# A rotation's 64 powers from two 8-entry tables instead of five doublings, in a hybrid S5, attention and mLSTM trunk

## Chip, cores and metric

The kernel runs on one core of a Trainium2 chip. The metric is the device time of one execution in microseconds (us): the median of three runs before the change is 1186.29 us, with runs from 1185.99 to 1187.22 us.

## The reference, cut to what matters

Two residual layers on a sequence of 512 positions and 1024 channels, all in float32. Layer 0 mixes with an S5 state-space head group and a dilated attention side by side, layer 1 with an mLSTM; a squared-ReLU MLP follows each. What the change touches is the S5 recurrence:

```python
lam_bar = jnp.exp(lam * dt)                       # 32 groups x 64 complex states
b_bar = ((lam_bar - 1.0) / lam)[..., None] * lax.complex(b_re, b_im)
bu = jnp.einsum('bsgc,gpc->bsgp', u32.astype(jnp.complex64), b_bar)
_, states = lax.associative_scan(s5_combine, (a_el, bu), axis=1)   # x[t] = lam_bar*x[t-1] + bu[t]
y = jnp.einsum('bsgp,gcp->bsgc', states, c).real + d * u32
```

The kernel cuts the 512 positions into 64 blocks of 8. Within a block everything is small matrices; between blocks the state is multiplied by lam_bar to the 8th power. That complex factor is split into its size (mag8) and its angle. The angle is taken out by a rotation with the powers 0 to 63 of the unit number cos + i sin of 8 angles, so that a real scan (size only) runs along the 64 blocks, and then put back. The change is about how these 64 powers are made.

## The kernel before

**Layout.** Activations lie as 8 tiles of 128 channels by 512 positions. Every projection weight block (a "unit", 128 x 1024 floats) is loaded by SP's queue and split in two parts whose sum is the weight: ScalarE copies the high part (`wh`, the line of copy_act, L120), VectorE subtracts to get the low part (`wl`, L96). TensorE multiplies three combinations (24 matmuls of 512 columns for a unit). There are two slots for `wh` and two for `wl` in layer 0, so a unit's copy can start when the unit that held its slot has been multiplied.

**Order of the work.** `EVEN_SEQ` is the hand-written order of layer 0's steps; a planner then reorders instructions by readiness, with the program's order as priority, and fixes each engine's queue. Each engine runs its queue strictly in that order. The start of the sequence is

```python
"u0 C0 a0 K0 E0 b0 u1 n0 T0 a2 C1 u2 E1 v0 v1 K1 C2 u3 E2 v2 B0 B1 v3 O0 ..."
```

The steps u, a, b, v are projections and take the weight units in this order: u0, a0, b0, u1, a2, u2, v0, v1, u3, v2, v3. The v steps share four PSUM accumulators, from v0 to the end of v3, and these four are all there are of that kind; u3, which comes before v2 in the order, needs one of them, so TensorE runs u3 after v3, and u3's split weight keeps its slot until then.

**S5.** The 32 groups are worked in four rounds Q of 8 groups: C (the powers for the input matrix), K (the same for the output, `CG`), T (matrices from them), E (the rotation), B (rotate, scan, rotate back), O (output). `s5_params` (called in the middle of the loading loop, before the sixth of the 8 `prep` calls) makes what all rounds share: `lrr`, `lsr`, `mag8`, the start values `e1`, and, with 25 small instructions on GpSimd (POOL), five repeated squarings of the unit number, `pr` and `pis`. After them POOL makes the tables `la` and `lb` for K.

`s5_rot` (step E) runs once for each round. It fills power 0, copies power 1, and then doubles the list five times: each doubling is two products and a sum on VectorE, followed (for the first four) by two ScalarE copies that swap the halves of the partitions, because real parts lie in partitions 0 to 63 and imaginary parts in 64 to 127 of `A`, and the other way round in `S`. The last step is four ScalarE copies of 64 x 512 from `A` into the tile `E`. `A` and `S` are the tiles x6 and x7, shared by all rounds.

Of the kernel before, what the change touches and what calls it, by code (L numbers as in the profile page):

```python
# [12 lines left out]
AF = mybir.ActivationFunctionType  # L13
ALU = mybir.AluOpType
AX = mybir.AxisListType

P = 128
# [44 lines left out]
class Trunk:  # L62
# [425 lines left out]
    def s5_params(self, pool):  # L488
        G = 32
        u = lambda name, shape=(P, G): self.t(pool, shape, "s5_" + name)  # L490
        lp = Slab([self.tmp("rA", bufs=1), self.tmp("rB", bufs=1), self.tmp("qs", bufs=1)])
        prm = self.prm
        are, aim, ldt = prm[:, 0], prm[:, 1], prm[:, 2]
        w = lambda name, shape=(P, G): lp.get(shape)
        dt = w("dt")
        self.exp_acc(lp, dt, ldt)
        z = w("z", (P, 2, G))
        th = w("th", (P, 2, G))
        self.mul(z[:, 0], are, dt)
        self.ts(z[:, 1], z[:, 0], 8.0, ALU.mult)  # L500
        self.mul(th[:, 0], aim, dt)
        self.ts(th[:, 1], th[:, 0], 8.0, ALU.mult)
        mag = w("mag", (P, 2, G))
        self.exp_acc(lp, mag, z)
        sn = w("sn", (P, 2, G))
        cs = w("cs", (P, 2, G))
        self.sincos(lp, sn, cs, th)
        lre = self.tmp("qv", bufs=1)[:, 0:9 * G].rearrange("p (i g) -> p i g", g=G)
        lim = self.tmp("sf")[:, 0:9 * G].rearrange("p (i g) -> p i g", g=G)
        lrr = u("lrr", (P, 8, G))  # L510
        lsr = u("lsr", (P, 8, G))
        self.nc.vector.memset(lre[:, 0], 1.0)
        self.nc.vector.memset(lim[:, 0], 0.0)
        self.mul(lre[:, 1], mag[:, 0], cs[:, 0])
        self.mul(lim[:, 1], mag[:, 0], sn[:, 0])
        for n in (1, 2, 4):
            mk = lp.mark()
            t1 = lp.get((P, n, G))
            t2 = lp.get((P, n, G))
            sr = lre[:, 1:1 + n]  # L520
            si = lim[:, 1:1 + n]
            br = lre[:, n:n + 1].to_broadcast([P, n, G])
            bi = lim[:, n:n + 1].to_broadcast([P, n, G])
            self.mul(t1, sr, br)
            self.mul(t2, si, bi)
            self.sub(lre[:, n + 1:2 * n + 1], t1, t2)
            self.mul(t1, sr, bi)
            self.mul(t2, si, br)
            self.add(lim[:, n + 1:2 * n + 1], t1, t2)
            lp.reset(mk)  # L530
        for j in range(8):
            self.copy_act(lrr[:, j], lre[:, 7 - j])
            self.act(lsr[:, j], lim[:, 7 - j], AF.Copy, scale=self.sgn)
        mag8 = u("mag8")
        self.copy_act(mag8, mag[:, 1])
        e1 = u("e1", (P, 2, G))
        self.copy_act(e1[0:64, 0], cs[0:64, 1])
        self.copy_act(e1[64:128, 0], sn[64:128, 1])
        self.copy_act(e1[0:64, 1], sn[0:64, 1])
        self.copy_act(e1[64:128, 1], cs[64:128, 1])  # L540
        pr = u("pr", (P, 5, G))
        pis = u("pis", (P, 5, G))
        gt = lambda o, x, y, op: self.nc.gpsimd.tensor_tensor(out=o, in0=x, in1=y, op=op)  # L543
        mk = lp.mark()
        t1 = lp.get((P, G))
        t2 = lp.get((P, G))
        for m in range(5):
            cr = cs[:, 1] if m == 0 else pr[:, m - 1]
            ci = sn[:, 1] if m == 0 else pis[:, m - 1]
            gt(t1, cr, cr, ALU.mult)  # L550
            gt(t2, ci, ci, ALU.mult)
            gt(pr[:, m], t1, t2, ALU.subtract)
            gt(t1, cr, ci, ALU.mult)
            gt(pis[:, m], t1, t1, ALU.add)
        lp.reset(mk)
        self.ts(pis, pis, self.sgn, ALU.mult)
        lm = w("lm")
        nr = w("nr")
        ni = w("ni")
        den = w("den")  # L560
        kre = w("kre")
        kim = w("kim")
        t1 = w("kt1")
        self.ts(lm, lre[:, 1], 1.0, ALU.subtract)
        gt(nr, lm, are, ALU.mult)
        gt(t1, lim[:, 1], aim, ALU.mult)
        gt(nr, nr, t1, ALU.add)
        gt(ni, lim[:, 1], are, ALU.mult)
        gt(t1, lm, aim, ALU.mult)
        gt(ni, ni, t1, ALU.subtract)  # L570
        gt(den, are, are, ALU.mult)
        gt(t1, aim, aim, ALU.mult)
        gt(den, den, t1, ALU.add)
        self.nc.vector.reciprocal(out=den, in_=den)
        gt(kre, nr, den, ALU.mult)
        gt(kim, ni, den, ALU.mult)
        krs, kis, kr, kn = w("krs"), w("kis"), w("kr"), w("kn")
        self.ts(krs, kre, self.sgn, ALU.mult, -1.0, ALU.mult)
        self.ts(kis, kim, self.sgn, ALU.mult, -1.0, ALU.mult)
        self.ts(kn, kim, -1.0, ALU.mult)  # L580
        la, lb = u("la", (P, 9, G)), u("lb", (P, 9, G))
        bk = lambda k: k.unsqueeze(1).to_broadcast([P, 9, G])
        t9 = lp.get((P, 9, G))
        gt(la, lre, bk(krs), ALU.mult)
        gt(t9, lim, bk(kis), ALU.mult)
        gt(la, la, t9, ALU.subtract)
        gt(lb, lre, bk(kn), ALU.mult)
        gt(t9, lim, bk(kre), ALU.mult)
        gt(lb, lb, t9, ALU.subtract)
        self.lrr, self.lsr = lrr, lsr  # L590
        self.mag8, self.e1, self.pr, self.pis = mag8, e1, pr, pis
        self.la, self.lb = la, lb

    def ypair(self, k):
# [2 lines left out]
    def xt(self, k):  # L597
        return self.t(self.cp, (P, T), f"x{k}", F32, 1)

    def s5_rot(self, pool, Q):  # L600
        nc = self.nc
        gs = slice(8 * Q, 8 * Q + 8)
        v3 = lambda t: t.rearrange("p (g k) -> p g k", k=64)
        A, S = v3(self.xt(6)), v3(self.xt(7))
        nc.vector.memset(A[0:64, :, 0:1], 1.0)
        nc.vector.memset(A[64:128, :, 0:1], 0.0)
        nc.vector.memset(S[0:64, :, 0:1], 0.0)
        nc.vector.memset(S[64:128, :, 0:1], 1.0)
        self.copy_act(A[:, :, 1], self.e1[:, 0, gs])
        self.copy_act(S[:, :, 1], self.e1[:, 1, gs])  # L610
        for m in range(1, 6):
            n = 1 << m
            b = lambda x: x[:, m - 1, gs].unsqueeze(2).to_broadcast([P, 8, n])
            w = self.t(pool, (P, 8, n), "w0")
            self.mul(A[:, :, n:2 * n], A[:, :, 0:n], b(self.pr))
            self.mul(w, S[:, :, 0:n], b(self.pis))
            self.add(A[:, :, n:2 * n], A[:, :, n:2 * n], w)
            if m < 5:
                self.copy_act(S[0:64, :, n:2 * n], A[64:128, :, n:2 * n])
                self.copy_act(S[64:128, :, n:2 * n], A[0:64, :, n:2 * n])  # L620
        E = self.t(pool, (P, 2, 8, 64), "E", bufs=2)
        self.copy_act(E[0:64, 0], A[0:64])
        self.copy_act(E[64:128, 0], A[0:64])
        self.act(E[0:64, 1], A[64:128], AF.Copy, scale=-1.0)
        self.copy_act(E[64:128, 1], A[64:128])
        self.s5e[Q] = E
# [772 lines left out]
```

## Time and profile before

| what | value |
|---|---|
| median of 3 runs | 1186.29 us |
| time of the profiled execution | 1185.93 us |
| its span | 1184.1 us |
| TensorE matmul busy | 1161.5 us (98%) |
| VectorE busy | 813.4 us (69%) |
| ScalarE busy | 643.1 us (54%) |
| GpSimd busy | 64.1 us (5%) |
| mean granted TensorE clock | 0.995 |

All times in the rows are microseconds from the span's start. In the rows PE is TensorE, DVE is VectorE, ACT is ScalarE, POOL is GpSimd. "acc<-wh,hg" reads: written tile acc, read tiles wh and hg. Layer 0's mixer ends near 220 us; the rest of the span holds the MLPs and the mLSTM layer, and the change does not touch them. The stage that matters lies between 38 and 140 us.

### The profile page before, as it was taken

To read this page: it belongs to the slowest core of one execution; us is meant where nothing else is said; L and a number is where in the kernel's file an instruction comes from. 1 tells how busy PE (TensorE), PEld (TensorE's weight loads), DVE (VectorE), ACT (ScalarE), POOL (GpSimd) and SP (SyncE) were. 2 spreads that over 40 slices of the span, in tenths; PEclk is the share of its full clock that TensorE was granted. 3 is DMA by queue.
4 is the path that set the end of the run, shared out by engine and by line. 5 is a ranking of instruction groups with operands and counts; after the bars stand their busy time and mean duration, and the time that the engine had idled before them with its cause. 6 is when DMAs were issued, how large, how long until landed. Compare 5 with 4: busy or idle time off the path is not lost.

```text
span 1184.1 us, 15701 instructions
## 1 busy us (share of the span) xinstructions
PE 1161.5 (98%) x5540; PEld 956.2 (81%) x5540; DVE 813.4 (69%) x1466; ACT 643.1 (54%) x1162; POOL 64.1 (5%) x121
## 2 busy tenths in 40 slices
PE   6989999999999999999999999999999999999998
PEld 5868776788888888888888888887888888888887
DVE  8799864666457447779858975865664574477796
ACT  5467777444434446666656645544444444456664
POOL 0522220000000000000100000000000000000000
PEclk9989999999999999999999999999999999999999
DMA  6434531359999335565624333222599994346654
GB/s 236 125 95 122 143 79 58 121 202 370 351 345 357 122 120 160 194 195 172 188 90 153 107 108 107 81 89 72 182 353 367 345 350 144 111 157 195 208 185 158
DMA packets 73869, 216.56 MB, mean 183 GB/s; under 512 B 16888, under 2 KB 17992, under 8 KB 73792
## 3 DMA queue, kind: packets, MB, share of 16 engines
q1 hardware_dynamic: 72576, 214.27, 53.7%
q0 software_dynamic: 1216, 1.31, 0.5%
q8 instruction: 43, 0.70, 0.2%
q14 instruction: 34, 0.28, 0.1%
HBM read 175.14 MB, written 38.31 MB: 180 GB/s over the span
## 4 chain that ended last, share of the span: by engine, by line
PE 92%; DVE 3%; ACT 1%; POOL 1%; issue 1%; DMA 1%; SPq 0%; DVEq 0%; ACTq 0%
PE acc L123 79%; PE psa L123 8%; PE psb L123 3%; DVE wl L96 1%; PE psb L898 1%; POOL rA L543 1%; PE psb L281 1%; ACT wh L120 0%; ACT hg L117 0%; DVE hg L108 0%; DMA hg<-in_amask 0%; DMA wr<-in_w_l 0%; DVE x L108 0%; PE psb L1207 0%; DVE x L96 0%
## 5 line engine op out<-in xcount | busy, mean ns | idle before, releaser
L123 PE MATMUL acc<-hg,wh 128*128 128x512 f32 x1600 | 500.7, 393 | 8.8 <-ACT hg L117 7.2
L120 ACT ACTIVATE wh<-wr 128x1024 fp32r<-128x1024 f32 x243 | 257.2, 1060 | 398.1 <-PE acc L123 321.3
L96 DVE TENSOR_TENSOR wl<-wr,wh 128x1024 fp32r<-128x1024 f32 x243 | 297.3, 1224 | 221.5 <-ACT wh L120 211.4
L123 PEld LDWEIGHTS acc<-hg,wh 128*128 128x128 f32 x1600 | 298.7, 188 | 70.1 <-ACT hg L117 7.2
L123 PE MATMUL acc<-hg,wl 128*128 128x512 f32 x800 | 313.6, 392 | 0.6 <-DVE wl L96 0.6
L123 PE MATMUL acc<-wh,sp 128*128 128x512 f32 x768 | 223.0, 389 | 0.0
L123 PEld LDWEIGHTS acc<-hg,wl 128*128 128x128 f32 x800 | 150.7, 188 | 31.9 <-DVE wl L96 1.1
L123 PEld LDWEIGHTS acc<-wh,sp 128*128 128x128 f32 x768 | 144.2, 188 | 30.0
L123 PE MATMUL acc<-wl,sp 128*128 128x512 f32 x384 | 135.9, 390 | 0.8 <-DVE wl L96 0.8
L120 ACT ACTIVATE sp<-s 128x256 fp32r<-128x256 f32 x224 | 89.8, 409 | 6.8 <-PE acc L123 5.7
L96 DVE TENSOR_TENSOR tq<-tq,tq 128x1024 f32<-128x1024 f32 x64 | 78.2, 1222 | 21.0 <-DMA tq<-in_w2s 20.0
L96 DVE TENSOR_TENSOR sp<-s,sp 128x256 fp32r<-128x256 f32 x224 | 86.8, 417 | 1.4 <-ACT sp L120 1.4
L123 PEld LDWEIGHTS acc<-wl,sp 128*128 128x128 f32 x384 | 71.9, 188 | 16.6 <-DVE wl L96 1.6
L123 PE MATMUL acc<-wh,hg 128*128 128x512 f32 x192 | 63.0, 402 | 5.4 <-ACT wh L120 5.4
L123 PEld LDWEIGHTS acc<-wh,hg 128*128 128x128 f32 x192 | 36.6, 193 | 13.2 <-ACT wh L120 5.8
L123 PE MATMUL psa<-wh,sp 128*128 128x512 f32 x128 | 42.0, 389 | 0.0
L117 ACT ACTIVATE rr<-acc 128x512 f32<-128x512 f32 x72 | 41.6, 578 | 0.0
L117 ACT ACTIVATE s<-rr 128x512 f32<-128x512 f32 x64 | 40.4, 631 | 1.0
L123 PE MATMUL acc<-wl,hg 128*128 128x512 f32 x96 | 38.5, 401 | 0.3 <-DVE wl L96 0.3
L108 DVE SCALAR_TENSOR_TENSOR sf<-zb,cvw,sf 128x512 f32<-128x512 f32 x48 | 35.3, 747 | 2.3 <-ACT sf L117 1.8
L96 DVE TENSOR_TENSOR x<-x,acc 128x512 f32<-128x512 f32 x16 | 10.8, 686 | 29.3 <-PE acc L123 29.2
L123 PE MATMUL acc<-y,wh 128*128 128x512 f32 x96 | 30.0, 394 | 0.0
(324 smaller groups left out, 1327.7 us busy)
## 6 DMA issues: line engine op xcount, KB each, us to landing
wr<-in_w_l SPq DMA_DIRECT2D x67, 512.0 KB, 3.5
wr<-in_w SPq DMA_DIRECT2D x64, 512.0 KB, 5.2
tq<-in_w2s SPq DMA_DIRECT2D x64, 512.0 KB, 6.3
T<-tq SPq DMA_DIRECT2D x64, 512.0 KB, 4.8
wr<-T SPq DMA_DIRECT2D x64, 512.0 KB, 3.3
wr<-in_w2s SPq DMA_DIRECT2D x48, 512.0 KB, 4.0
x<-in_xT SPq DMA_DIRECT2D x16, 256.0 KB, 4.1
na<-scr SPq DMA_DIRECT2D x8, 256.0 KB, 3.7
```

What stands on the lines that cost most here:

```text
L96: return self.nc.vector.tensor_tensor(out=o, in0=x, in1=y, op=op)
L108: return self.nc.vector.scalar_tensor_tensor(out=o, in0=x, scalar=s, in1=y, op0=op0, op1=op1)
L117: return self.nc.scalar.activation(o, x, f, bias=bias, scale=scale, **kw)
L120: return self.nc.scalar.activation(o, x, AF.Copy)
L123: return self.nc.tensor.matmul(o, l, r, start=start, stop=stop)
L281: self.nc.tensor.transpose(p[:, k * P:(k + 1) * P], self.x[4 * n + k][:, t * P:(t + 1) * P], self.ident)
L543: gt = lambda o, x, y, op: self.nc.gpsimd.tensor_tensor(out=o, in0=x, in1=y, op=op)
L898: self.nc.tensor.transpose(t[:, k * P:(k + 1) * P], p[:, k * P:(k + 1) * P], self.ident)
```

## The change

The start values `e1` and the doublings in `s5_rot` go. `s5_params` keeps the five squarings on POOL (now called `sqr` and `sqi`, in temporary space) and calls the new `s5_tabs`, which makes, once for all 32 groups, a table of the powers 0 to 7 (`C8`, `S8`) and a table of the powers 0, 8, ..., 56 (`T1`, `T2`), each by two doublings with half swaps. Each round then forms its 64 powers as two products of 512 elements, one with each pair of tables, and their sum. Scratch is in the tiles x0 and x1.

```diff
-        e1 = u("e1", (P, 2, G))
-        self.copy_act(e1[0:64, 0], cs[0:64, 1])
         ...
-        self.ts(pis, pis, self.sgn, ALU.mult)
+        self.s5_tabs(pool, cs, sn, sqr, sqi)
+    def s5_tabs(self, pool, cs, sn, sqr, sqi):
+        self.ts(sqi, sqi, self.sgn, ALU.mult)
+        ...
+        for k, A, S, c, s in ((0, A8, S8, cs[:, 1], sn[:, 1]), (1, self.T1, S64, sqr[:, 2], sqi[:, 2])):
+            nc.vector.memset(A[up, :, 0:1], 1.0)
+            nc.vector.memset(A[dn, :, 0:1], 0.0)
+            nc.vector.memset(S[up, :, 0:1], 0.0)
+            nc.vector.memset(S[dn, :, 0:1], 1.0)
+            sc = lambda h: 1.0 if k == 0 else self.sgn[h]
+            self.copy_act(A[up, :, 1], c[up])
+            self.act(A[dn, :, 1], s[dn], AF.Copy, scale=sc(dn))
+            self.act(S[up, :, 1], s[up], AF.Copy, scale=sc(up))
+            self.copy_act(S[dn, :, 1], c[dn])
+            for m in (1, 2):
+                n = 1 << m
+                i = m - 1 + 3 * k
+                b = lambda x: x[:, i].unsqueeze(2).to_broadcast([P, G, n])
+                self.mul(A[:, :, n:2 * n], A[:, :, 0:n], b(sqr))
+                self.mul(tm[:, :, 0:n], S[:, :, 0:n], b(sqi))
+                self.add(A[:, :, n:2 * n], A[:, :, n:2 * n], tm[:, :, 0:n])
+                self.copy_act(S[up, :, n:2 * n], A[dn, :, n:2 * n])
+                self.copy_act(S[dn, :, n:2 * n], A[up, :, n:2 * n])
+        self.copy_act(self.C8[up], A8[up])
+        ...
+        self.act(self.T2, S64, AF.Copy, scale=self.sgn)
     def s5_rot(self, pool, Q):
-        for m in range(1, 6):
-            n = 1 << m
-            b = lambda x: x[:, m - 1, gs].unsqueeze(2).to_broadcast([P, 8, n])
-            w = self.t(pool, (P, 8, n), "w0")
-            self.mul(A[:, :, n:2 * n], A[:, :, 0:n], b(self.pr))
-            self.mul(w, S[:, :, 0:n], b(self.pis))
-            self.add(A[:, :, n:2 * n], A[:, :, n:2 * n], w)
-            if m < 5:
-                self.copy_act(S[0:64, :, n:2 * n], A[64:128, :, n:2 * n])
-                self.copy_act(S[64:128, :, n:2 * n], A[0:64, :, n:2 * n])
+        A, W = self.xt(6), self.xt(7)
+        ta = lambda t: t[:, gs].unsqueeze(3).to_broadcast([P, 8, 8, 8])
+        tb = lambda t: t[:, gs].unsqueeze(2).to_broadcast([P, 8, 8, 8])
+        self.mul(v4(A), ta(self.T1), tb(self.C8))
+        self.mul(v4(W), ta(self.T2), tb(self.S8))
+        self.add(A, A, W)
```

## Rows read from the trace of the kernel before

**Rows 1.** The page's first part: busy time, share of span, instructions.
```profile
PE 1161.5 (98%) x5540; PEld 956.2 (81%) x5540; DVE 813.4 (69%) x1466; ACT 643.1 (54%) x1162; POOL 64.1 (5%) x121
```

**Rows 2.** TensorE's waits, 0 to 212 us: total, times, longest.
```profile
PE acc L123 <- ACT wh L120: 5.4, 1, 5.4
```

**Rows 3.** Chain of waits in order of time: start us, us, what.
```profile
38.15 0.43 POOL rA L543 x2
...
91.81 5.48 PE acc L123 x24
...
134.26 3.82 DMA hg<-in_amask
```

**Rows 4.** Busy by stretch: length, PE, PEld, DVE, ACT, POOL, PEclk, DMA, GB/s.
```profile
60.00:70.00 10.00, 4.34 (x10) 2.86 (x10) 9.84 (x28) 5.19 (x12) 3.08 (x2) 0.68 0.27 77
70.00:100.00 30.00, 30.00 (x196) 25.57 (x195) 28.52 (x71) 22.35 (x46) 6.46 (x12) 0.99 0.40 120
100.00:134.00 34.00, 34.00 (x207) 30.01 (x207) 33.57 (x72) 23.70 (x43) 5.57 (x6) 1.00 0.49 138
```

**Rows 5.** TensorE timeline: start us, us, instruction, count, [idle before <-releaser].
```profile
59.79 0.39 PE L123 MATMUL acc<-wh,hg 128*128 128x512 f32 x1
65.57 2.07 PE L123 MATMUL acc<-wh,hg 128*128 128x512 f32 x4 [5.39 <-ACT wh L120]
67.91 0.79 PE L123 MATMUL acc<-wl,hg 128*128 128x512 f32 x1 [0.27 <-DVE wl L96]
...
73.48 0.39 PE L123 MATMUL acc<-wh,hg 128*128 128x512 f32 x1
...
75.31 1.04 PE L649 MATMUL psb<-cst,Z 128*128 128x128 f32 x8
```

**Rows 6.** ScalarE timeline, 53 to 66 us.
```profile
53.51 0.47 ACT L120 ACTIVATE x<-x 64x32 f32<-64x32 f32 x2 [1.59 <-DVE x L96]
55.99 0.52 ACT L120 ACTIVATE x<-x 64x64 f32<-64x64 f32 x2 [2.01 <-DVE x L96]
57.84 0.63 ACT L120 ACTIVATE x<-x 64x128 f32<-64x128 f32 x2 [1.32 <-DVE x L96]
...
59.07 1.04 ACT L120 ACTIVATE wh<-wr 128x1024 fp32r<-128x1024 f32 x1
61.27 1.27 ACT L120 ACTIVATE E<-x 64x512 f32<-64x512 f32 x2 [1.16 <-DVE x L96]
...
64.47 1.04 ACT L120 ACTIVATE wh<-wr 128x1024 fp32r<-128x1024 f32 x1
```

**Rows 7.** GpSimd timeline, 53 to 64 us.
```profile
53.46 0.82 POOL L543 TENSOR_TENSOR s_la<-qv,rB 128x288 f32<-128x288 f32 x1
...
59.08 3.16 POOL L800 TENSOR_TENSOR qky<-qkv,pwh 128x16 f32<-128x16 f32 x1 [1.43 <-DVE qkv L108]
62.22 0.86 POOL L543 TENSOR_TENSOR s_lb<-s_lb,rB 128x288 f32<-128x288 f32 x1
```

**Rows 8.** VectorE timeline, 48 to 73 us.
```profile
48.51 0.30 DVE L112 TENSOR_SCALAR s_pis<-s_pis,cst 128x160 f32<-128x160 f32 x1 [0.81 <-POOL s_pis L543]
...
55.99 0.80 DVE L96 TENSOR_TENSOR x<-x,s_pr 128x128 f32<-128x128 f32 x1
...
60.82 0.41 DVE L96 TENSOR_TENSOR x<-x,w 128x256 f32<-128x256 f32 x1
...
65.35 0.17 DVE L96 TENSOR_TENSOR x<-x,s_pr 128x16 f32<-128x16 f32 x1
...
68.94 0.22 DVE L96 TENSOR_TENSOR x<-x,s_pr 128x64 f32<-128x64 f32 x1
...
69.21 0.68 DVE L96 TENSOR_TENSOR w<-bin,s_lsr 128x512 f32<-128x512 f32 x1
...
70.55 0.28 DVE L96 TENSOR_TENSOR x<-x,s_pr 128x128 f32<-128x128 f32 x1
...
71.62 0.55 DVE L96 TENSOR_TENSOR Z<-Z,w 128x384 f32<-128x384 f32 x1
72.09 0.41 DVE L96 TENSOR_TENSOR x<-x,s_pr 128x256 f32<-128x256 f32 x1
```

More of the change, by code (lines that the diff above doesn't have):

```diff
@@ L535, in s5_params @@
         self.copy_act(mag8, mag[:, 1])
-        e1 = u("e1", (P, 2, G))
-        self.copy_act(e1[0:64, 0], cs[0:64, 1])
[L538 to L542, printed above, removed]
         gt = lambda o, x, y, op: self.nc.gpsimd.tensor_tensor(out=o, in0=x, in1=y, op=op)
+        sqr, sqi = w("sqr", (P, 5, G)), w("sqi", (P, 5, G))
         mk = lp.mark()
@@ L547, in s5_params @@
         for m in range(5):
-            cr = cs[:, 1] if m == 0 else pr[:, m - 1]
-            ci = sn[:, 1] if m == 0 else pis[:, m - 1]
+            cr = cs[:, 1] if m == 0 else sqr[:, m - 1]
+            ci = sn[:, 1] if m == 0 else sqi[:, m - 1]
             gt(t1, cr, cr, ALU.mult)
             gt(t2, ci, ci, ALU.mult)
-            gt(pr[:, m], t1, t2, ALU.subtract)
+            gt(sqr[:, m], t1, t2, ALU.subtract)
             gt(t1, cr, ci, ALU.mult)
-            gt(pis[:, m], t1, t1, ALU.add)
+            gt(sqi[:, m], t1, t1, ALU.add)
         lp.reset(mk)
-        self.ts(pis, pis, self.sgn, ALU.mult)
+        self.s5_tabs(pool, cs, sn, sqr, sqi)
         lm = w("lm")
@@ L590, in s5_params @@
         self.lrr, self.lsr = lrr, lsr
-        self.mag8, self.e1, self.pr, self.pis = mag8, e1, pr, pis
+        self.mag8 = mag8
         self.la, self.lb = la, lb
@@ L598, in xt @@
         return self.t(self.cp, (P, T), f"x{k}", F32, 1)
+    def s5_tabs(self, pool, cs, sn, sqr, sqi):
+        nc, G = self.nc, 32
+        tab = lambda name: self.t(pool, (P, G, 8), "s5_" + name)
+        self.C8, self.S8, self.T1, self.T2 = [tab(n) for n in ("c8", "s8", "t1", "t2")]
+        up, dn = slice(0, 64), slice(64, 128)
+        self.ts(sqi, sqi, self.sgn, ALU.mult)
+        w3 = self.xt(0).rearrange("p (n g e) -> p n g e", n=2, e=8)
+        A8, S8 = w3[:, 0], w3[:, 1]
+        w3 = self.xt(1).rearrange("p (n g e) -> p n g e", n=2, e=8)
+        S64, tm = w3[:, 0], w3[:, 1]
+        for k, A, S, c, s in ((0, A8, S8, cs[:, 1], sn[:, 1]), (1, self.T1, S64, sqr[:, 2], sqi[:, 2])):
[18 more added lines that the diff above has]
+        self.copy_act(self.C8[up], A8[up])
+        self.copy_act(self.C8[dn], S8[dn])
+        self.copy_act(self.S8[up], S8[up])
+        self.copy_act(self.S8[dn], A8[dn])
+        self.act(self.T2, S64, AF.Copy, scale=self.sgn)
@@ L600, in s5_rot @@
     def s5_rot(self, pool, Q):
-        nc = self.nc
         gs = slice(8 * Q, 8 * Q + 8)
[L603 to L610, printed above, removed]
@@ L611, in s5_rot @@
-        for m in range(1, 6):
-            n = 1 << m
-            b = lambda x: x[:, m - 1, gs].unsqueeze(2).to_broadcast([P, 8, n])
-            w = self.t(pool, (P, 8, n), "w0")
-            self.mul(A[:, :, n:2 * n], A[:, :, 0:n], b(self.pr))
-            self.mul(w, S[:, :, 0:n], b(self.pis))
-            self.add(A[:, :, n:2 * n], A[:, :, n:2 * n], w)
-            if m < 5:
-                self.copy_act(S[0:64, :, n:2 * n], A[64:128, :, n:2 * n])
-                self.copy_act(S[64:128, :, n:2 * n], A[0:64, :, n:2 * n])
+        v4 = lambda t: t.rearrange("p (g a b) -> p g a b", a=8, b=8)
@@ L621, in s5_rot @@
+        A, W = self.xt(6), self.xt(7)
[4 more added lines that the diff above has]
+        self.add(A, A, W)
+        A = A.rearrange("p (g k) -> p g k", k=64)
         E = self.t(pool, (P, 2, 8, 64), "E", bufs=2)
```

## The prediction, made before the change was run

> **What bounds the kernel now.** Read the busy shares first: TensorE is busy for 98% of the span [rows 1], so anything that the change saves on VectorE or ScalarE counts only where TensorE stands still. Read TensorE's waits next, over layer 0's mixer. Apart from the start-up, one wait stands out: 5.4 us, once, for a weight copy on ScalarE [rows 2]. Then find it in TensorE's timeline: a matmul at 59.79, and the next group at 65.57, 5.39 us idle [rows 5]. The four matmuls after it take 2.07 us, and the granted clock in that stretch of ten is 0.68 of full speed [rows 4]: idle time at the full 2.4 GHz, then matmuls at 1.2 GHz. The unit concerned (v2, by the order of the steps) runs from 65.57 to 73.87 [rows 5], 8.3 us, where a unit of 24 matmuls at full speed takes 5.48 us [rows 3]. So the place costs 5.4 + 2.8 = 8.2 us.
>
> Now ask what ScalarE did. v2's copy can't start before v1's matmuls end, at 60.18 (its slot was v1's; the other slot is kept by u3). It started at 64.47 [rows 6]. Ahead of it in the queue stood the four copies into E of round 0, which began at 61.27 after waiting for VectorE [rows 6]; these waited for the last sum of round 0's doublings, at 60.82 [rows 8]. So round 0's rotation, as it stands in ScalarE's queue ahead of a weight copy, holds TensorE for 64.47 - 60.2 = 4.3 of the 5.4 us. The remaining 1.1 us is the copy itself.
>
> After it TensorE is busy without a gap from 70 to 134 (30.00 of 30, 34.00 of 34) with VectorE at 28.52 and 33.57 beside it [rows 4]. At 134.26 the chain goes through the load of the attention mask, 3.82 us, into the tile that the projections read [rows 3]. It moves with the last projection, so time won at 60 us is kept to the end unless VectorE takes it back on the way.
>
> **The change, part by part.** Each number of us below is a duration; neighbours on VectorE overlap by some 0.08 us, so the sums for it are upper ends.
>
> Removed on VectorE, for each round: 15 products and sums in five sizes, of which rows 8 have 16, 64, 128 and 256 elements: 0.17, 0.22, 0.28, 0.41 us. The 32-element size lies between the first two, 0.19 (an estimate). Three of each: 3 x 1.27 = 3.8 us, 15.2 us in four rounds. Added: in each round three operations of 512, at 0.68 for a product with a broadcast operand of that size [rows 8], 8.2 us in all; and the tables, once, two levels for each of two tables, three operations a level, of 64 and 128 elements: 6 x (0.22 + 0.28) = 3.0 us. VectorE comes out 4.0 us shorter. Sixteen fills go and eight come; a small gain, left at nothing. All of it lies under TensorE's matmuls, except as it moves round 0.
>
> Removed on ScalarE: in each round four pairs of copies, 0.47, 0.52 and 0.63 for the last three [rows 6], and about 0.45 for the first (an estimate from the 64x32 pair), with two start copies: some 2.5 us, 10 us in all, and four for e1. Added: eight base copies of 64x32 (0.24 each), four copies of 64x64 (0.26) and four of 64x128 (0.32): 4.2 us; four of 64x256 and one of 128x256, which no row shows: between 0.32 and 0.64 each [rows 6], I take 0.4 for its nearness to 64x128: 2.0 us. ScalarE is 4 to 5 us shorter, hidden too: it is busy for 22.35 of 30 us [rows 4].
>
> Moved: everything above except the squarings waits for POOL's last square, which VectorE's sign product shows at 48.51 [rows 8]; POOL starts the squares at 38.15 [rows 3], and the change leaves their count. The tables can't begin in earnest before 48.8. From there to E in round 0: before, five levels deep, 48.8 to 61.2. After, two levels for two tables side by side (each about product 0.28, product 0.28, sum 0.28, two copies 0.6, so 1.3 us a level at most), the last ScalarE copies for C8, S8 and T2 (2.0 us), two products and a sum (2.0 us): 48.8 + 2.6 + 2.0 + 2.0 = 55.4. The price of two weight operations in between is 1 to 2 us. So round 0's A is ready at 55 to 58 instead of 61.2, and its four copies into E (2.5 us, twice the pair of rows 6) end at 57.5 to 60.5, about when v1 frees its slot.
>
> POOL's part is uncertain. While it makes la (53.46) a VectorE product of 128 elements took 0.80 us [rows 8], against 0.28 at 70.55. The new products of round 0 fall in that time: nothing lost below (if they come before), 3 x 0.5 us and two levels more above; I take 1 us, inside the 55 to 58.
>
> The Trainium skill has a rule on this (SBUF, "Who interferes with whom"): a VectorE instruction with two inputs in SBUF contends with a GpSimd instruction that reads SBUF, and the later one waits. The trace agrees with the 0.80 against 0.28 just named. By the rule all fifteen operations up to A would wait, some 15 x 0.5 = 7.5 us, which speaks against this change and leads to the second rival.
>
> **The sum.** v2's copy at 60.2, 1.04 long, first matmul at 61.35 instead of 65.57: 4.2 us. Four matmuls (0.9 us) need the high part alone; the low part comes from VectorE, 1.2 us after the copy plus what stands in its queue, so about 1 us of waiting. With a gap of 1 us in place of 5.4 I take full clock. v2 ends at 61.35 + 5.5 + 1.0 = 67.8 instead of 73.87: 6.0 us won. What is late next: the transposes of round 1's Z, on TensorE at 75.31 [rows 5], whose last sum VectorE finished at 72.17 [rows 8]. That is a slack of 3.1 us against 6.0 us of advance; VectorE gets some 1.5 us earlier by then. I let it take back 1.5 us (between nothing and 3). Gain 4.5 us: 1185.93 for the profiled execution becomes 1181.4; the median of the runs lies 0.36 above that execution, so 1181.8.
>
> **Rivals.** *Hidden anyway.* Round 1's rotation is now short too. It can start when round 0's copies have left A (58 to 60), and its four copies stand earlier in the program than v2's weight copy. If the planner puts them ahead of it, ScalarE waits for round 1 as it did for round 0: copies from 61 or 62, weight copy from 63.5 to 64.5, TensorE at 64.6 to 65.6, low clock as before. For it: the two become ready within a microsecond of each other. Against: VectorE has the products of K for round 0 in its queue just then. Gain 0 to 1.5 us: 1184.8 to 1186.5.
>
> *Slower.* The same order in ScalarE's queue, but round 1's sum sits behind K's products on VectorE, and these wait for POOL's lb, which stands behind the power function: 59.08 + 3.16, then lb to 63.08 [rows 7]. Then round 1's A is ready at 64.5 to 66, its copies end at 67 to 68.5, and TensorE starts v2 at 68 to 69.6, 2.5 to 4 us later than now. It decides from the point where round 1's sum ends after 64.4 us (64.4 + 2.5 us of copies + 1.04 of weight copy is 68). Time 1188.5 to 1190.5. For it: contention with POOL that the planner may not foresee, as in round 0 now. Against: 4.0 us less work on VectorE, and products of 0.68 instead of a chain of fifteen with halts between.
>
> **How the numbers follow.** The forecast, with its own range of 1179 (nothing taken back, 0.3 us of waiting) to 1183.5 (3 us taken back): 0.48. Hidden anyway: 0.30. Slower: 0.22. The order of other steps can shift by the new plan too, some 1 us either way. A range from 1178.5 to 1188.9 leaves out most of the slow case and a little below. About 0.2% (2.4 us) is what a measurement of this kernel can tell from no change. Faster by more than that: the forecast and a little of the first rival, 0.50; within: 0.27; slower: 0.23.
>
> **What would show it.** In TensorE's timeline the wait between v1 and v2 shrinks from 5.4 to 1 or 2 us, with full clock after it; on ScalarE v2's weight copy starts at 60 to 61, with round 0's E copies ahead of it and round 1's behind it; VectorE has the sum of round 0 before 58. It is wrong if the four E copies of round 1 stand ahead of that weight copy, if the wait stays above 4 us, or if TensorE, busy without a gap from 70 to 134 now, shows waits for Z or CG there that sum to more than 3 us.

## The result and the profile after

The changed kernel takes 1199.74 us (median of four runs, 1197.99 to 1200.53) where the kernel before took 1186.76 beside it: ratio 1.0108, 95% interval 1.009 to 1.0125. That is 13.0 us slower. The prediction said 1181.8 and gave 0.23 to slower. The profiled execution took 1200.53 us, its span is 1198.8, its mean granted clock 0.988 against 0.995.

The first part of the page of after answers to [rows 1]:

```profile
PE 1169.2 (98%) x5540; PEld 962.2 (80%) x5540; DVE 812.8 (68%) x1422; ACT 643.2 (54%) x1141; POOL 72.0 (6%) x121
```

VectorE lost 44 instructions and 0.6 us, ScalarE 21 instructions and nothing. TensorE's work is the same 5540 matmuls, yet its busy time rose by 7.7 us: these are matmuls at a lower clock. TensorE's waits of after, 0 to 212 us (total, times, longest), answer to the single row of [rows 2]:

```profile
PE psb L916 <- ACT hg L117: 4.8, 4, 3.7
PE acc L123 <- DVE wl L96: 4.7, 1, 4.7
PE acc L123 <- ACT wh L120: 4.1, 3, 2.1
```

One wait became three places (the wait at the start-up aside, 7.7 us here and 7.2 before). The two for weight parts (`wl`, `wh`) are in TensorE's timeline of after (start, us, instruction, [idle before <- releaser]), which answers to [rows 5]:

```profile
61.15 0.39 PE L123 MATMUL acc<-wh,hg 128*128 128x512 f32 x1
62.68 1.20 PE L123 MATMUL acc<-wh,hg 128*128 128x512 f32 x4 [1.15 <-ACT wh L120]
68.53 0.80 PE L123 MATMUL acc<-wl,hg 128*128 128x512 f32 x1 [4.66 <-DVE wl L96]
...
74.33 0.39 PE L123 MATMUL acc<-wh,hg 128*128 128x512 f32 x1
...
79.30 2.08 PE L123 MATMUL acc<-wh,hg 128*128 128x512 f32 x4 [2.08 <-ACT wh L120]
```

v2 starts 2.9 us earlier than before, as meant, and then waits 4.66 us for its low part. It ends at 74.72, 0.85 later than before. v3 then waits for its weight copy. ScalarE's timeline of after, which answers to [rows 6], has the cause of the second wait:

```profile
59.52 0.51 ACT L117 ACTIVATE s_t<-x,cst 128x256 f32<-128x256 f32 x1
61.57 1.06 ACT L120 ACTIVATE wh<-wr 128x1024 fp32r<-128x1024 f32 x1 [1.54 <-PE acc L123]
65.84 1.27 ACT L120 ACTIVATE E<-x 64x512 f32<-64x512 f32 x2 [3.21 <-DVE x L96]
...
75.10 0.63 ACT L120 ACTIVATE rr<-qky 128x512 f32<-128x512 f32 x1 [6.72 <-POOL qky L818]
75.64 1.25 ACT L120 ACTIVATE E<-x 64x512 f32<-64x512 f32 x2
...
78.19 1.06 ACT L120 ACTIVATE wh<-wr 128x1024 fp32r<-128x1024 f32 x1
```

v2's copy (61.57) stands ahead of round 0's E copies, and the tables' last copy is done at 60.0. But `rr`, a copy of the first norm, waits 6.72 us for GpSimd, and round 1's E copies and v3's weight copy stand behind it. GpSimd's timeline of after, beside [rows 7]:

```profile
54.65 0.81 POOL L536 TENSOR_TENSOR s_la<-qv,rB 128x288 f32<-128x288 f32 x1 [0.38 <-DVE rB L113]
...
64.81 10.26 POOL L818 TENSOR_TENSOR qky<-qkv,pwh 128x16 f32<-128x16 f32 x1 [5.26 <-DVE qkv L108]
```

The power function took 10.26 us where it took 3.16. VectorE's timeline of after, beside [rows 8], shows why round 0 and the low part are late:

```profile
49.60 0.23 DVE L96 TENSOR_TENSOR x<-x,rB 128x64 f32<-128x64 f32 x1
...
54.72 0.83 DVE L96 TENSOR_TENSOR x<-x,rB 128x64 f32<-128x64 f32 x1
...
58.87 1.24 DVE L96 TENSOR_TENSOR x<-s_t,s_c 128x512 f32<-128x512 f32 x1
...
65.13 0.68 DVE L96 TENSOR_TENSOR x<-x,x 128x512 f32<-128x512 f32 x1
...
67.27 1.21 DVE L96 TENSOR_TENSOR wl<-wr,wh 128x1024 fp32r<-128x1024 f32 x1
```

A table product of 64 elements took 0.83 us beside GpSimd's `la` and 0.23 before it; a product of 512 took 1.24 instead of 0.68. The two table levels lasted from 49.60 to 58.83, and round 0's sum ended at 65.81. v2's low part, whose copy was done at 62.6, stands at 67.27 behind K's products, round 0's rotation and a first product of round 1's.

Where the rest goes is read by stretch. After (length, then busy time of PE, PEld, DVE, ACT, POOL, then clock, DMA share, GB/s), to be set against [rows 4]:

```profile
60.00:70.00 10.00, 4.20 (x15) 2.79 (x14) 10.00 (x20) 3.60 (x6) 5.18 (x1) 0.73 0.20 58
70.00:100.00 30.00, 27.92 (x153) 22.83 (x152) 23.97 (x42) 17.26 (x28) 9.61 (x9) 0.86 0.31 91
100.00:134.00 34.00, 34.00 (x181) 30.10 (x180) 27.26 (x48) 19.65 (x32) 7.49 (x9) 0.90 0.45 130
134.00:160.00 26.00, 21.53 (x141) 17.28 (x140) 19.85 (x44) 19.01 (x38) 6.17 (x3) 0.87 0.38 112
```

From 100 to 134 TensorE is never idle, in both kernels, and still the clock is 0.90 instead of 1.00. TensorE's timeline of after around 112 us:

```profile
107.94 0.33 PE L123 MATMUL psb<-U,DT 128*128 128x64 f32 x2
...
111.46 0.34 PE L123 MATMUL psb<-cst,ev 128*128 128x4 f32 x2
...
112.10 0.36 PE L123 MATMUL psb<-cst,rr 128*128 128x4 f32 x2
...
113.48 0.57 PE L123 MATMUL psb<-cst,rr 128*128 128x4 f32 x2
113.91 0.77 PE L123 MATMUL acc<-hg,wh 128*128 128x512 f32 x1
```

32 matmuls of 64 columns (step O0) and 16 of 4 columns (the sums of a norm) stand back to back, and within them the pair of 4 columns goes from 0.36 to 0.57 us. The kernel before has the same matmuls at 97.13 to 104, but with seven of 512 columns among those of 4, and its clock stayed at 1.00. Two of its lines:

```profile
100.84 0.48 PE L123 MATMUL acc<-hg,wh 128*128 128x512 f32 x1
...
103.58 0.36 PE L123 MATMUL psb<-cst,ev 128*128 128x4 f32 x2
```

The third place is the attention, at 148 to 157 us. ScalarE's timeline of after:

```profile
148.72 1.28 ACT L117 ACT_TABLE_LOAD   x1
...
151.02 1.28 ACT L117 ACT_TABLE_LOAD   x1
152.32 0.63 ACT L117 ACTIVATE x<-x 128x512 f32<-128x512 f32 x1
...
154.16 1.28 ACT L117 ACT_TABLE_LOAD   x1
```

And TensorE's timeline of after, three matmuls that wait for such an exponential:

```profile
156.22 0.55 PE L916 MATMUL psb<-cst,hg 128*128 128x128 f32 x3 [3.67 <-ACT hg L117]
```

The Gelu of step O1 (152.32) fell between the attention's exponentials, so a table was loaded three times, and TensorE waits 3.67 us. ScalarE of before has one load there, its Gelu ahead of it:

```profile
137.24 0.62 ACT L117 ACTIVATE x<-x 128x512 f32<-128x512 f32 x1
...
139.83 1.28 ACT L117 ACT_TABLE_LOAD   x1
```

To compare runs I sum, over stretches of 2 us, TensorE's idle time and its busy time times (1 - granted clock), for the first 216 us. Us, for each stretch:

| kernel | 0-60 | 60-76 | 76-90 | 90-130 | 130-160 | 160-216 | sum | span |
|---|---|---|---|---|---|---|---|---|
| before | 8.9 | 7.9 | 0 | 0 | 2.8 | 0.8 | 20.3 | 1184.1 |
| after | 9.7 | 7.3 | 5.0 | 3.4 | 7.6 | 1.0 | 34.0 | 1198.8 |
| after, the repeat below | 8.9 | 8.0 | 3.0 | 1.7 | 8.9 | 1.0 | 31.5 | 1198.0 |

The place that the change aimed at gains 0.6 us; three others, 15 to 90 us further on, lose 13.2. The sum differs by 13.7, the span by 14.7. In the repeat the place gains nothing, and the three others lose 10.8: where the loss falls varies by some 2 us between runs of one plan.

### The profile page after: what moved, and what is told of

Read it like the earlier page. It is cut to its first block, busy times and chain, and to the rows that moved or that the text cites. A ratio compares the mean times of both kernels' runs of the same rounds, so it can differ in the third digit from the quotient of the medians.

```text
span 1198.8 us, 15633 instructions
## 1 busy us (share of the span) xinstructions
PE 1169.2 (98%) x5540; PEld 962.2 (80%) x5540; DVE 812.8 (68%) x1422; ACT 643.2 (54%) x1141; POOL 72.0 (6%) x121
## 4 chain that ended last, share of the span: by engine, by line
PE 91%; DVE 3%; ACT 3%; POOL 2%; DMA 1%; issue 1%; SPq 0%; DVEq 0%; ACTq 0%; POOLq 0%
PE acc L123 78%; PE psa L123 8%; PE psb L123 3%; POOL qky L818 1%; DVE wl L96 1%; ACT hg L117 1%; PE psb L916 1%; ACT wh L120 1%; PE psb L281 1%; POOL rB L536 0%; DMA wr<-in_w_l 0%; DVE CG L96 0%; ACT L117 0%; DVE x L108 0%; PE psb L1225 0%
## 5 line engine op out<-in xcount | busy, mean ns | idle before, releaser
L96 DVE TENSOR_TENSOR x<-x,acc 128x512 f32<-128x512 f32 x16 | 10.8, 687 | 29.2 <-PE acc L123 29.2
```

The lines of the kernel that those rows point to most:

```text
L96: return self.nc.vector.tensor_tensor(out=o, in0=x, in1=y, op=op)
```

## Experiments

Two theories at first. *Order*: the new plan of all queues places other work badly (the norm ahead of E, O0's narrow matmuls together, Gelu between exponentials), and the loss is there. *Own work*: building tables or the wider rotation ends later than the doublings, and the loss follows from that, in any order. Ratios are to the kernel before on the same chip, with their 95% intervals.

**The changed kernel once more, and the first norm's root on VectorE.** The second keeps the first norm's power function off GpSimd:

```diff
-        if self.PPOW:
+        if self.PPOW and (i, isk) != (0, 0):
```

> The changed kernel once more, unaltered; its first profile has the loss in three places: v2's low part waits 4.66 us behind VectorE's products, POOL's power for n0 takes 10.26 us instead of 3.16 and holds v3's high copy in ScalarE's queue (v3 ends 6.0 us late), and round 1's Gelu falls between two exps (attention 3.7 us later). Theory (three places): 1198 to 1201 us, with the same waits. For the power's 10.26 us: if it is what this stretch of VectorE's products does to POOL, 9 to 11 us again; if it was a chance, 3 to 6 us, and then v3 ends 3 to 5 us earlier and the time is 1194 to 1197.

> The changed kernel with n0's inverse root taken on VectorE instead of as POOL's power; all else as in the changed kernel. Theory (three places): round 1's E copies no longer stand behind the wait for the power, they run when round 1's sum is there (70.6 us), v3's high copy at about 73, its 2.1 us wait and the slow clock of 80 to 90 go: v3 ends near 84 instead of 88.6, the time is 1194 to 1196. Rival (building the tables is what costs, the power only stands beside it): 1198 to 1201, no change. Rival (any new order of the plan costs this much): no change either.

The repeat: 1198.72 (1.0096, 1.0081 to 1.0111), with the 10.26-us power function and waits of 1.15, 4.77 and 1.50 us at v2 and v3; the time of a plan repeats. Without the power function v3's wait is gone, as expected, but the kernel takes 1203.73 (1.0139, 1.0122 to 1.0156). The plan changed again: TensorE waits 3.7 us before 135.26 for a copy of T, and behind that wait stand O1's narrow matmuls, the sums of norms and the attention. This stretch, in the columns of the stretches above, has no idle time and half the clock:

```profile
140.00:160.00 20.00, 20.00 (x95) 17.22 (x95) 13.66 (x32) 12.25 (x22) 6.11 (x2) 0.50 0.21 53
```

So a repaired wait was paid for elsewhere, and more. My number was missed, and from here on each run is read by all its stretches.

**O1 before b1, taking the Gelu out of the attention.**

```diff
-... r2 E3 a3 b1 B3 O1 K3 b3
+... r2 E3 a3 O1 b1 B3 K3 b3
```

> The changed kernel with step O1 three steps earlier in the order (a3 O1 b1 B3 in place of a3 b1 B3 O1), so that round 1's Gelu is ready before the first exp; seven table loads up to the end of layer 0's attention in place of nine. Theory (three places): the loss at the start of attention (the offset goes from 9.2 to 12.8 us there) goes, v2 and v3 stay late: 1195 to 1197. Rival (the attention absorbs it, its start is bound by the projections alone): 1199 to 1201.

1194.39 (1.0059, 1.0044 to 1.0074), 0.6 below what I expected. The Gelu no longer lies between the exponentials; the stretch 130 to 160 loses 4.6 us instead of 7.6 and 8.9. But 76 to 90 loses 0.7 instead of 5.0 and 3.0, and 60 to 76 loses 9.0, so not all of the gain is the Gelu's. The wait for v2's low part stays (4.8).

**Tables filled by one copy each.**

```diff
-        for k, A, S, c, s in (...): ... (the two doublings of each table)
+        b = lambda x: x.unsqueeze(2).to_broadcast([P, 32, 8])
+        for x, y in ((self.C8, sqr[:, 0]), (self.S8, sqi[:, 0]), (self.T1, sqr[:, 4]), (self.T2, sqi[:, 4])):
+            self.copy_act(x, b(y))
```

> The changed kernel with the four tables filled by one ScalarE copy each straight from the squarings, in place of the two doublings with half swaps (leaves out the building of the powers: the rotation's values are not those of the reference). Everything after the tables is as changed; the tables come some 5 us earlier. Theory (building the tables puts round 0's and round 1's products right in front of v2's low part, and the rest follows): round 0's sum before 58, v2's low part less than 1.5 us late, no long wait for v3's high copy: 1180 to 1188, so faster than before or level with it. Rival (the two products of 512 elements a round, and the power beside them, cost the time): 1195 to 1200.

This leaves out the building of the powers, so the rotation's values are not the reference's. 1193.55 (1.0052, 1.0032 to 1.0072), between the two expectations: even with tables that cost next to nothing the kernel is slower than before. v2 still waits 2.7 us for its high and 3.0 for its low part; the power function takes 3.36.

**u3 behind v3**, so that v2's weight has a free slot early (and u3's input in the free tile x1); on after and on before:

```diff
-... K1 C2 u3 E2 v2 B0 B1 v3 O0 ...
+... K1 C2 E2 v2 B0 B1 v3 u3 O0 ...
```

> The changed kernel with projection u3 (its weight too) after v3 in the order, where TensorE runs it anyway, and u3's lifted input in the free tile x1 instead of x5: u3's split weight no longer keeps the slot, so v2's high and low parts are made while v0 and v1 are multiplied. Theory (the loss is what stands in front of v2's and v3's split weights): the waits of 4.7 and 1.5 to 2.1 us and the two half-clock stretches behind them go, and the plan has no Gelu between exps; the half-clock stretch near 112 to 118, behind the matmuls of 64 and 4 columns that stand together, stays: 1183 to 1188. Rival (the tables and the two 512-element products cost this time wherever they stand): 1195 or more.

> The kernel before with the same move of u3: v2's wait of 5.4 us and the half clock behind it go, which alone gives 1178 to 1181. But in its plan some 20 us of matmuls of 4 to 128 columns stand together ahead of the attention. Theory for the clock (it falls in such a run though TensorE is busy all the time, as in the changed kernel at 112 to 118): half clock over 10 to 20 us there, 1185 to 1190. Rival (the clock falls only behind waits): 1178 to 1181.

After: 1194.58 (1.0065, 1.005 to 1.008), above the 1183 to 1188 that I expected. The waits of v2 and v3 are gone but for 0.8, and a wait of 4.0 appears at 80.02 for copies that stand in ScalarE's queue behind `rr` and E. Before: 1194.38 (1.0058, 1.004 to 1.0076), above what I expected: v2 waits 2.8 instead of 5.4, but a wait of 3.2 and half clock come at 134 to 151. The old rotation too, given a gain at v2, loses it with another plan.

**Before, with the tables built and used by nobody.** `s5_tabs` is called in `s5_params` where the changed kernel calls it, with `pr` and `pis`; the doublings stay.

> The kernel before with the tables built as well and used by nothing (its doublings do all the work). Theory (what costs is the order that the plan takes around v2, v3 and the exps, not the table work itself): 1184 to 1191, v2's wait 4 to 7 us. Rival (building the tables, some 25 small VectorE operations and 21 ScalarE copies just ahead of v2, is the loss): 1194 or more.

1198.01 (1.0094, 1.0079 to 1.011), my miss again: as slow as the change, though the rotations are the old ones. v2 waits 1.9 and 4.0, the power function takes 8.32 us, and 6.1 us are lost at 130 to 160. It does not tell the building from the order that the building brings.

**The power function by itself**: eleven of them on GpSimd, each beside another stretch of VectorE work.

> A kernel by itself (computes nothing of the reference): eleven times POOL's power on 128 x 16, each with another VectorE stretch beside it: none; K's products and sums of 384; the new rotation's products and sum of 512; the mix that stood beside the power in the changed kernel; the same with the E copies on ScalarE; 40 products of 128; rotation products alone; sums alone; low-part subtractions; the mix again; none. Theory (the long gapless stretch with the rotation's products starves POOL): about 3.2 us with none and with K's products, 8 us or more in the mix, as long as the stretch. Rival (it is something of that place in the kernel, not VectorE): about 3.2 us in all.

```profile
8.48 2.90 POOL L75 TENSOR_TENSOR qky<-qkv,pwh 128x16 f32<-128x16 f32 x1 [7.64 <-DVE qkv L74]
...
79.97 3.81 POOL L75 TENSOR_TENSOR qky<-qkv,pwh 128x16 f32<-128x16 f32 x1 [6.85 <-DVE qkv L74]
```

These are one of the shortest and the longest, from GpSimd's timeline. A VectorE busy with products does not by itself make it 10 us: as I had put it, the theory fell. But the long ones have something in common that I had overlooked. In after the function lasts from 64.81 to 75.07, and VectorE beside it ends its long run of instructions with

```profile
71.61 0.68 DVE L96 TENSOR_TENSOR w<-bin,s_lsr 128x512 f32<-128x512 f32 x1
72.33 0.69 DVE L96 TENSOR_TENSOR Z<-Z,w 128x512 f32<-128x512 f32 x1
```

Up to 72.29 each of these instructions starts before the one ahead of it has ended; there VectorE is free for 0.04 us, for the first time since the function began, and the function ends 2.78 us later. The three other runs with 10.25 or 10.26 us and the one with 8.32 end 2.77 or 2.78 us behind the first such gap too; with VectorE idle the function takes 2.90 (the line at 8.48). So the long times read as a wait for a gap on VectorE. No run was made on this, and four of the eleven took 3.14 to 3.32 us though VectorE left no gap beside them; what let these in is not shown.

**The order by itself.** TensorE's first 563 matmuls are held in a listed order by edges that add no semaphore; the planner does the rest. After in before's order, and before in after's order:

```diff
+        for x, y in zip(PE_ORDER, PE_ORDER[1:]):
+            self.tc.add_manual_dep(pe[y], pe[x].name, free, reason="PE order")
```

> The changed kernel, whole, with one thing held: TensorE's first 563 matmuls (all of layer 0's mixer up to where the two plans agree again) are queued in exactly the order of the kernel before; the other engines are planned freely around that. Theory now (the loss is the new plan, above all TensorE's order: matmuls of 4 and 64 columns together at half clock, the Gelu between exps, v3 behind the power): the half-clock stretches near 112 to 118 and 146 to 160 go, 1184 to 1190. Rival (the change's own work, tables and products, costs it by holding v2's and v3's split weights): 1194 to 1199.

> The kernel before, whole, with TensorE's first 563 matmuls queued in the order of the changed kernel. Theory (order): at least two thirds of the loss comes without the change: 1194 to 1200, with half clock near 112 to 118 and Gelu between exps. Rival (the change's own work): 1185 to 1189.

| | before's TensorE order | after's TensorE order |
|---|---|---|
| doublings | 1186.47 | 1195.96 (1.0083, 1.0066 to 1.01) |
| tables | 1191.12 (1.0035, 1.0022 to 1.0049) | 1199.74, again 1198.72 |

Read across (the kernel before had 1186.5 to 1187.2 beside them): the order costs 9.5 us with the old rotation and 7.6 to 8.6 with the new. Read down: the change costs 4.7 and 2.8 to 3.8 with TensorE's order held. The other queues were planned anew in every cell, so this second part is the change's own work together with the new order of those queues, and the first is TensorE's order with what the others do around it. Both theories hold a part, TensorE's order the larger. In the run with before's order the Gelu stands ahead of the exponentials, and the narrow matmuls at 90 to 130 cost nothing. Of the 4.0 us that are left in the sums (table below), 1.7 are at 130 to 160 and 1.7 at v2, where ScalarE shows the cause:

```profile
65.10 1.27 ACT L125 ACTIVATE E<-x 64x512 f32<-64x512 f32 x2 [1.90 <-DVE x L101]
...
67.67 1.06 ACT L125 ACTIVATE wh<-wr 128x1024 fp32r<-128x1024 f32 x1
```

These are lines of its ScalarE timeline. v2's copy stands behind round 0's E as in the kernel before, and now that sum ends at 65.07, so TensorE waits 7.7 us instead of 5.4. In the other kernel, the old rotation in after's order, the waits are these:

```profile
PE acc L128 <- ACT wh L125: 6.9, 1, 6.9
PE psb L903 <- ACT hg L122: 3.4, 3, 3.0
```

**v2's copies put first.** Before's TensorE order, and edges that put v2's high part ahead of `rr` and round 0's E, and its low part ahead of K's second products; on after and before, the rest planned anew.

> The changed kernel with TensorE's first 563 matmuls in the order of the kernel before and, new, v2's split weight put first: on ScalarE v2's high copy ahead of n0's rr copy and round 0's four E copies, on VectorE v2's low part ahead of round 0's second product and sum and of K's lb products of rounds 0 and 1. This is the order that the prediction took for granted. Theory (order alone decides, the prediction's place was right): v2 waits under 2 us, full clock, v3 as before: 1180 to 1184, the predicted 1181.8. Rival (the change's own work then comes late somewhere else, B0 or B1 or the attention): 1186 to 1191.

> The kernel before, doublings and all, with the same order: TensorE's own first 563 matmuls held, v2's high copy ahead of n0's rr copy and round 0's E copies, v2's low part ahead of K's lb products of rounds 0 and 1. Theory (the 8 us of that place belong to the order of two queues, not to how the powers are made): 1180 to 1184, level with the changed kernel under the same order. Rival (only the tables make room for it): 1186 to 1190.

Both came out above both of their expectations. After: 1192.31 (1.0046, 1.0032 to 1.006); v2 waits 1.1 and 1.4, and then Z makes TensorE wait 4.3 and a norm 3.4. Before: 1197.11 (1.0086, 1.0072 to 1.0099), with 2.9 at v2 and 6.2 for a Z later. This is the one pair in which the new rotation is the faster, and it is a pair of different plans.

**All three queues held.** TensorE's 563, ScalarE's 240 and VectorE's 300 first instructions are listed (before's own order, and for after that of the run with before's TensorE order) with two moves: v2's high part ahead of round 0's E copies (in after ahead of `rr` too), and the low parts of u3 and v2 ahead of the last two of K's first products (in after, the last three).

> The kernel before with its whole plan held (TensorE's first 563, ScalarE's first 240, VectorE's first 300 instructions in its own order) but for two moves: v2's high copy ahead of round 0's E copies, and the low parts of u3 and v2 ahead of the last two of K's first products. Theory (that place is worth what the prediction said, whatever makes the powers, and nothing is re-planned): v2 waits about 1 us for its high part, 0 to 2 for the low, full clock, its matmuls end at 67 to 69 instead of 73.9; what follows waits for VectorE's K0 and Z for 1 to 3 us: 1182 to 1185. Rival (VectorE's queue is the bound from 58 to 76 us, all is given back): 1186 to 1188.

> The changed kernel with the plan that it had under TensorE's order of before (1191.1 us) held in the same three queues, but for the same two moves: v2's high copy ahead of the rr copy and round 0's E copies, the low parts of u3 and v2 ahead of K's second three products. Theory (the order of this place): its wait falls from 7.7 to about 1 us, v2's matmuls end at 68 to 70 instead of 77, 1 to 3 us come back as waits for VectorE: 1184 to 1187, so not faster than before. Rival (VectorE bound): 1190 to 1192.

Before with the moves: 1185.55 (0.9988, 0.9979 to 0.9997). It beats both kernels, by 1.4 us the one before (the interval is 0.4 to 2.5). TensorE there:

```profile
61.45 1.20 PE L130 MATMUL acc<-wh,hg 128*128 128x512 f32 x4 [1.15 <-ACT wh L127]
64.56 0.50 PE L130 MATMUL acc<-wl,hg 128*128 128x512 f32 x1 [1.92 <-DVE wl L103]
```

After with the moves: 1192.01 (1.0039, 1.0026 to 1.0051). Its TensorE:

```profile
62.25 1.20 PE L130 MATMUL acc<-wh,hg 128*128 128x512 f32 x4 [1.15 <-ACT wh L127]
...
67.95 0.39 PE L130 MATMUL acc<-wh,hg 128*128 128x512 f32 x1
71.72 1.08 PE L130 MATMUL psa<-CG,bin 128*32 128x128 f32 x16 [3.38 <-DVE CG L103]
...
76.19 1.94 PE L674 MATMUL psb<-cst,Z 128*128 128x128 f32 x8 [1.49 <-DVE Z L103]
```

And VectorE of the same kernel, the last sum of that Z:

```profile
75.49 0.55 DVE L103 TENSOR_TENSOR Z<-Z,w 128x384 f32<-128x384 f32 x1
```

v2 runs as forecast, full clock and its end at 68.34, and then TensorE stands 3.38 us for CG and 1.49 for Z at half clock. VectorE finishes Z at 76.04, where it did at 72.17 [rows 8]: products and sums of 512 elements for rounds 0 to 2 stand between K's and Z's.

**CG and Z put first as well** (VectorE: Z, K and v3's low part ahead of the rotations; ScalarE: v3's copy ahead of E), on both; and then also round 0's B and the copies behind it earlier, on both.

> The changed kernel, three queues held as in hold_a, and what TensorE waits for next put in its order too: on VectorE behind v2's low part first K's products for round 0, then round 1's Z, then v3's low part, and only then the sums and products of the rotations and K for round 1; on ScalarE v3's high copy ahead of the E copies, and the copies of BT ahead of round 1's E copies. Theory (VectorE's order was what gave the gain back): v2 ends near 68.3 as in hold_a, the waits of 3.4 and 1.5 us behind it and their half clock go, v3 ends 4 to 6 us earlier than before: 1180 to 1185. Rival (VectorE has too much work there in any order, round 0's rotation and B are late then): 1187 to 1192.

> The kernel before with the same order of VectorE's and ScalarE's work from v2's split weight to round 1's rotation: u3's low part before round 0's last sum, v2's right behind it, then K for round 0, Z, v3's low part, then K's first products and the doublings of round 1; copies of v3's high part and BT ahead of round 1's last half swaps. Theory (the order is worth its gain with the old rotation too): 1180 to 1184, level with hold_a2 or faster. Rival (it needs the new rotation): 1186 or more.

> hold_a2 with the next wait taken on: on VectorE round 0's B right behind round 1's sum, round 2's rotation behind it; on ScalarE the copy that frees a sum of v (and so lets u3 start) ahead of B's copies and round 1's E copies. Theory (it is order all the way, the change is worth its 4 to 5 us once the order is right): the wait of 8.7 us falls to 1 or 2, v3's advance of 5 us is kept: 1181 to 1186. Rival (each wait taken away comes back one step further on, because VectorE is full there): 1188 to 1194.

> hold_b2, the kernel before, with the same: round 0's B early on VectorE, the copy that frees a sum ahead of round 1's E copies. Theory (order all the way): the wait of 5.2 us falls to 1 or 2: 1181 to 1186, level with hold_a3. Rival (each wait comes back further on): 1187 to 1192.

First step: 1194.69 (1.0069, 1.0057 to 1.0082) and, with doublings, 1191.34 (1.004, 1.0026 to 1.0053). TensorE of the first: v3 is done at 77.8, and then comes the largest wait of all:

```profile
77.41 0.40 PE L130 MATMUL acc<-wh,hg 128*128 128x512 f32 x1
77.64 1.67 PE L130 MATMUL psa<-U,BT 128*128 128x64 f32 x14
88.06 1.22 PE L130 MATMUL acc<-hg,wh 128*128 128x512 f32 x2 [8.75 <-ACT x L124]
```

The rotations that were put off are wanted by B, whose copies (86.10) stand ahead of the copies that free TensorE's accumulators. Second step: 1195.29 (1.0066, 1.0048 to 1.0084) and 1189.51 (1.0021, 1.0012 to 1.0029). With tables the 8.75 became 1.4 and 2.1 (with doublings 5.2 became 1.4 and 3.1), and the 2.1 at 96.03 was followed by half the clock up to 113, in a stretch that is busy for 23.71 of 26 us:

```profile
90.00:116.00 26.00, 23.71 (x97) 20.48 (x96) 21.05 (x37) 14.38 (x24) 7.48 (x9) 0.67 0.47 136
```

Each wait taken away came back further on, with either rotation, and none of these six runs came within the range of its theory. What was won at v2 could not be kept beyond 1.4 us, and that with the doublings. In each of these three pairs, held by the same rules, the tables are 3.4 to 6.5 us slower. That VectorE is simply full there, as the rivals say, is not shown: from 60 to 100 us it was busy for 33.6 to 36.9 of 40 us in the three kernels with tables, and for 36.6 to 39.6 with doublings.

| kernel | 0-60 | 60-76 | 76-90 | 90-130 | 130-160 | 160-216 | sum | span |
|---|---|---|---|---|---|---|---|---|
| root on VectorE | 9.2 | 7.2 | 0 | 3.4 | 15.6 | 2.0 | 37.5 | 1201.9 |
| after in before's order | 8.8 | 9.6 | 0 | 0 | 4.5 | 1.4 | 24.3 | 1189.3 |
| before in after's order | 8.8 | 9.4 | 0 | 1.7 | 7.6 | 1.4 | 29.0 | 1193.5 |
| all held, tables | 9.1 | 7.3 | 3.1 | 0 | 4.4 | 1.4 | 25.3 | 1191.3 |
| all held, doublings | 8.4 | 5.0 | 0 | 0 | 3.0 | 0.8 | 17.3 | 1183.0 |

## Why the prediction was wrong

- *What bounds the kernel; the price of the place* (8.2 us): right. 7.9 us by the table above, and v2's high part came as forecast behind the end of v1, with 1.15 us of waiting.
- *"The order of other steps can shift by the new plan too, some 1 us either way"*: **this step failed.** With the old rotation, after's order of TensorE (the other queues planned around it) costs 9.5 us. It was costed from nothing: I followed the queues only up to 75 us, and the plan moved O0, a norm and a Gelu at 107 to 157 us. The forecast allowed for 1 us either way of it, the runs show nine. It is not the only one: with before's order held, the changed kernel still took 1191.12, 4.7 us longer and not 4.5 shorter, and that lies in the next two steps and the low part's.
- *"round 0's A is ready at 55 to 58"*: **this failed too**, 65.8, and 65.1 with before's order. Two terms were too small. The two levels took 9.2 us instead of 2.6: by the eleven table operations I add up from 49.60 on, the five beside GpSimd's products took 3.7 us instead of 1.3, and a low part, a product from PSUM and two Z products (3.5 us) stood among them. Then the three operations of 512 took from 58.87 to 65.81, because K's first six products (2.89) and another low part were between.
- *VectorE 4.0 us shorter, ScalarE 4 to 5*: 0.6 and nothing. On VectorE the tables' 2.4 us and the first product's 0.56 beside GpSimd take most of it back. On ScalarE two further table loads (2 x 1.28) take back half; for the rest I have no row.
- The contention that the Trainium skill names (SBUF, "Who interferes with whom") is in the trace: 0.83 against 0.23. Taken for all fifteen operations, as I took its rule, it gives 7.5 us; in after six were slowed, by 3.0 us, those that ran while GpSimd made `la` and `lb` (54.65 to 59.56). The rule spoke against the change rightly, and my 1 us was too small.
- *"about 1 us of waiting" for the low part*: 4.66. The rule of thumb "1.2 us after the copy plus what stands in its queue" was right, and I did not list the queue.
- *"I let it take back 1.5 us (between nothing and 3)"*: with everything held, 3.38 and 1.49 at half clock. So v2's end at 67.8 (measured 68.34) was right and worth nothing. I noted a slack of 3.1 us at Z and took VectorE to be earlier there; in that kernel it was 3.9 us later.
- *Rivals*: the slower case had the sign but not the place. Round 1's E copies did not go ahead of v2's weight copy, but ahead of v3's. Its condition, round 1's copies ahead of v2's behind a sum that ends after 64.4, came true nowhere here. The nearest is the kernel with before's order: there round 0's copies stood ahead of v2's, behind round 0's sum at 65.07, and TensorE waited 7.7 us (1191.12; the rival said 1188.5 to 1190.5).
- *What would show it wrong*: "if the wait stays above 4 us" came true, as 1.15 and 4.66 us for v2's two parts. "Waits for Z or CG there that sum to more than 3 us" came only where the order was held.

**Open.** The first norm's power function takes 10.25 or 10.26 us in four runs (the changed kernel twice, O1 early, u3 behind v3) and 8.32 in one, and 2.90 to 3.81 in all others, the eleven by themselves among them. The long times end at a gap on VectorE; why the short ones need none is not shown. In the changed kernel and its repeat it sets v3's wait, but removing it gained nothing. How much of the 2.8 to 6.5 us that are left with the order held is the tables' building, how much the wider products and how much the order of VectorE's and ScalarE's queues was not separated: the run with filled tables had yet another plan.

## What to carry to other kernels

Where a planner fixes the queues, an edit's price is its own work plus a new order of everything behind it, and here the second was about twice the first: hold the order of the engines by ordering edges, and time work and order apart, before an edit is judged. Shorter work on an engine is worth its place in the queue, not its length: list what stands between the first instruction that the edit moves and the one that the bounding engine waits for. A wait that moves on each time it is removed is a sign to look at a second engine (VectorE here, at 28.52 of 30 us in the kernel before) ahead of the next repair; how little can be gained then, the runs must say, here 1.4 us.

## What the runs showed of the hardware

- The granted clock fell without any wait at 112 to 119 us in after, at the end of 48 matmuls of 64 and 4 columns back to back, to 0.50, the level of 1.2 GHz. It did so in all seven runs in which these 48 stand together, towards their end or up to 2 us behind it, and stayed there for some 6.8 us in two of them and 3.4 in five, the repeat of after and the old rotation in after's order among these. In before, the same narrow matmuls with seven of 512 columns among them ran at 1.00. And where the clock had fallen at a wait, it stayed there while narrow matmuls followed: with the root on VectorE from 136 to 158, busy throughout, 11.0 us lost behind a wait of 3.7; in the second step with tables 8.5 us behind a wait of 2.1. In these two what follows the wait decides its price.
- GpSimd's power function of 128x16 took 2.90 us beside an idle VectorE and 8.32 to 10.26 in five runs, and in all five it ended 2.77 or 2.78 us behind the first gap between VectorE's instructions.
- A switch between Gelu and exponential costs ScalarE a load of 1.28 us each way; one Gelu among the exponentials cost TensorE 3.67 us of waiting.
